# A two-layer diffusion step on one core: first norm, DeltaNet gate rounds and last products rearranged

## The chip, the cores and the metric

The kernel runs on one core of a Trainium2 chip. The core has five engines with a queue each: TensorE (PE, matmuls and transposes; PEld are its weight loads), VectorE (DVE), ScalarE (ACT), GpSimd (POOL) and SyncE (SP, which only starts DMA transfers). The metric is the device time of one execution in microseconds (us), the median of several runs. The rows below come from one profiled execution of the kernel before.

## What is computed

Two groups of tokens, 128 context tokens and 512 latent ones, run through two layers of width 1024 that share their weights: an attention layer, then a gated DeltaNet layer, each followed by a squared-ReLU MLP. What matters here, cut from the reference:

```python
def rms_norm(x, gain):
    y = x * lax.rsqrt(jnp.mean(x * x, axis=-1, keepdims=True) + EPS)
    return y * gain

def modulation(cond, w_mod, b_mod):                 # w_mod[l]: 1024 x 6144
    m = jax.nn.silu(cond) @ w_mod + b_mod
    return jnp.split(m[..., None, :], 6, axis=-1)   # shift1, scale1, gate1, shift2, ...

def trunk_layer(x, mods, gain1, gain2, w1, w2, mixer):
    shift1, scale1, gate1, shift2, scale2, gate2 = mods
    mix, aux = mixer(rms_norm(x, gain1) * (1 + scale1) + shift1)
    x = x + gate1 * mix
    h = rms_norm(x, gain2) * (1 + scale2) + shift2
    return x + gate2 * (jnp.square(jax.nn.relu(h @ w1)) @ w2), aux

def delta_mixer(h, ...):                            # 8 heads
    qkv, z, a, b = split(h @ w_in)                  # q, k, v: conv, SiLU; q, k normalised
    o = forward scan + backward scan                # chunked delta rule, per head
    o = rms_norm(o, norm_gain) * silu(z)            # z gates the head's output
    return o @ w_out

y = rms_norm(x, final_norm)                         # at the end, for both groups
```

## The kernel before

All 640 tokens are handled together: x is kept feature-major, 8 tiles of 128 features x 640 tokens. Matmuls take an fp32 operand as the sum of two halves: `split` has ACT write the rounded value (hi) and DVE or POOL the rest (lo), and `mm3` makes three matmuls of the two pairs. Tiles come from pools by tag: tag x has 12 slots, h and a 16 each, all of 128x640; `raw` has three and `wpair` six of 4 KB per partition. The code is handed to a scheduler that fixes the order of the instructions of each engine before the run; an engine works through its own list and waits at each row for what that row needs. SP's list of transfers is such a list too.

The stages, in the order of the program (`run`, L1322):

1. **The head.** Five token blocks of x are loaded (`xin`), `transpose_x` (L482) turns them feature-major with 40 PE transposes and 8 DVE copies, squares each x tile on ACT and adds the squares on DVE. Five pairs of PE matmuls with a column of ones give the sums per token, `finish_rstd` makes 1/rms of them on DVE (`rsy`), and PE spreads that over a PSUM tile (`big<-c,rsy`), called r0 here. Beside that, `modulate(0, 0, fetch_slots)` (L398) multiplies the two condition vectors with the first third of `w_mod[0]`: 32 transfers of 256 KB into slots of the tags h and a, 32 matmuls `mod<-...` of 512 columns; four of them stand at four places of the PE array (q = 0 to 3). `modulation` (L415) copies the result on ACT (`x<-mod`), transposes it back on PE and adds the bias and makes the gain on DVE. `columns` (L389) transposes the small constant vectors. `key_weights` (L572) splits the weights of the keys, one half on POOL and one on DVE, and those of query head 0 on POOL.
2. **The first norm**, `first_norm` (L506): DVE makes `us` = x * r0 (`a<-x,big`, 8 of 640 columns). Then, for three token segments (128, 256 and 256 tokens, each group with its own gain and shift) and 8 features each: a TENSOR_SCALAR u * gain + shift in place, ACT's rounded copy to hi, and the difference lo. For features 2 and 5 (f % 3 == 2) POOL does the first and the last step, else DVE.
3. **Attention.** Keys are made first (`attn_kv`, L578): 5 blocks of 24 matmuls `pd<-w,h` 128x256, which need all 24 tiles of h, block by block. The second third of `w_mod[0]` comes in through the `raw` slots, which the value weights hold before; its matmuls `S<-raw,c` are put between those of the keys. Then values, eight query heads, output.
4. **MLP 0**, then **DeltaNet** (`delta`, L1244) in rounds r = 0 to 10: round r weaves `dn_dense(r)`, `dn_decay(r-1)`, `dn_inverse(r-2)`, `dn_scan(r-3)` and `gated(ZROUNDS[r])`. `gated` makes z of a head (`dn_z`, 48 matmuls `pd<-h,w` 128x320, two ACT evacuations `x<-pd` 128x320 with SiLU) and then `dn_out` (L1221): ACT squares, a DVE chain, a product on POOL, five PE transposes, a DVE product, and a transfer to DRAM or a split. A head's output o stays in an a slot from its scan to its `dn_out`. In rounds 8 to 10 the other two thirds of `w_mod[1]` are woven in (`pd<-raw,c`, `pd<-a,c`).
5. **MLP 1**, with `final(0)` in the middle and `final(1)` at the end (L1398): for three token blocks, PE transposes two halves of 512 columns each; the first half is scaled by `rsy` and the final gain on DVE in one instruction, the second on ACT and then POOL. The transfers out stand on ACT's queue (first halves) and on SP's (second halves).

Of the kernel before, what the change touches and what calls it, by code (L numbers as in the profile page):

```python
# [15 lines left out]
P = 128  # L16
# [22 lines left out]
RSQRT_SEED = float(0x5F3759DF)  # L39
ZROUNDS = {6: (0,), 7: (1,), 8: (2, 3), 9: (4, 5), 10: (6, 7)}  # L40
MODS = (6, 6, 6)
# [78 lines left out]
class Model:  # L120
# [342 lines left out]

    def fetch_slots(self, src):
        out = []
        for i in range(4):
            r = self.main("h" if i < 2 else "a", shape=[P, 512])
            self.nc.sync.dma_start(out=r, in_=src[:, i * 512 : (i + 1) * 512])
            out.append(r)
        return out  # L470
# [10 lines left out]

    def transpose_x(self, xs, x):  # L482
        for f in range(FT):
            x.append(self.main("x"))
            ps = self.ps("big", 2, 1024)
            for b in range(NBLK):
                self.tr(ps[:, b * P : (b + 1) * P], xs[b][:, f * P : (f + 1) * P])
            self.nc.vector.tensor_copy(out=x[f], in_=ps[:, :T])
            sq = self.main("x")
            self.act(sq, x[f], AF.Square)  # L490
            if f == 0:
                acc = sq
            else:
                self.tt(acc, acc, sq, ALU.add)
            yield
        cols = self.ps("nps", 1)[:, :NBLK]
        for b in range(NBLK):
            self.mm(cols[:, b : b + 1], acc[:, b * P : (b + 1) * P], self.one_col)
        r = self.finish_rstd(cols)
        out = self.ps("big", 2, 1024)  # L500
        for b in range(NBLK):
            self.mm(out[:, b * P : (b + 1) * P], r[:, b : b + 1].to_broadcast([P, P]), self.ident)
        self.r0 = out[:, :T]
        yield

    def first_norm(self, x, gm):  # L506
        us = [self.main("a") for _ in range(FT)]
        for f in range(FT):
            self.tt(us[f], x[f], self.r0, ALU.mult)
        drain(gm)  # L510
        h = self.new_h()
        gain, mods = self.gains[0][0], self.mods[0]
        for s, e, g in FIRST:
            for f, (hi, lo) in enumerate(h):
                eng = self.nc.gpsimd if f % 3 == 2 else self.nc.vector
                u = us[f][:, s:e]
                self.ts(u, u, gain[:, f, g : g + 1], ALU.mult, mods[:, f, g : g + 1], ALU.add, eng=eng)
                self.act(hi[:, s:e], u, AF.Copy)
                self.tt(lo[:, s:e], u, hi[:, s:e].bitcast(F32), ALU.subtract, eng)
        return h  # L520
# [51 lines left out]
    def key_weights(self):  # L572
        v, g = self.nc.vector, self.nc.gpsimd
        self.kw = self.kv_weights(self.kv_raw(QW), lambda: self.wtile([P, 4, 256]), 4, (g, v))
        self.vraws = self.kv_raw(QW + KVH * P)
        self.q0 = self.pair(self.a["attn_w_in"][0], 0, 0, eng=g)

# [744 lines left out]
    def run(self):  # L1322
# [3 lines left out]
        FC = [f * P for f in range(FT)]  # L1326
        with psum("ps0") as self.pq:
            xs = self.load_x()
            self.setup()
            gm = self.modulate(0, 0, self.fetch_slots)  # L1330
            x = []
            tx = self.transpose_x(xs, x)
            for _ in range(FT):
                next(gm)
                next(tx)
            drain(tx)
            self.columns()
            self.key_weights()
            h = self.first_norm(x, gm)
        with pool("attn") as self.ph:  # L1340
# [36 lines left out]
        with pool("mlp1") as self.ph, psum("ps5") as self.pq:  # L1377
# [20 lines left out]
            def final(half):  # L1398
# [12 lines left out]
                for i, b in enumerate(blocks):  # L1411
                    y = self.wp.tile([P, D], F32, tag="wpair", bufs=self.NW, name=self.nm("y"))
                    for c in range(0, D, 512):
# [3 lines left out]
                        out = y[:, c : c + 512]  # L1417
                        if c == 0:
                            self.stt(out, ps, r[:, i : i + 1], gain[:, c : c + 512], ALU.mult, ALU.mult)
# [49 lines left out]
```

## Time and profile before

| | |
|---|---|
| runs shown | 1884.30, 1886.86, 1880.81 us; median 1884.3 us |
| the profiled execution, its own time | 1883.34 us |
| its span, first to last instruction | 1881.5 us (1.8 us of the time lie around it) |
| busy | PE 1793.3 us, DVE 991.3, ACT 753.9, POOL 311.6 |
| mean granted clock of TensorE | 0.984 of full speed |

The profile gives the start and length of each instruction on its engine, grouped where alike ones follow each other, and in brackets how long the engine stood idle before and whose work ended that. PEclk is the granted clock of TensorE: 1.00 is 2.4 GHz and 0.50 is 1.2 GHz. The span is nearly full of PE work, so the places of interest are those where PE has none: the head, short gaps in the DeltaNet rounds, and the tail.

### The profile page before, as it was taken

The numbers are of one execution on the slowest core, as the hardware profiler recorded it, in microseconds if no ns is written. First come the engines' busy times: TensorE is split into PE (matmuls) and PEld (weight loads), VectorE is DVE, ScalarE is ACT, GpSimd is POOL, SyncE is SP. The second block draws the span as 40 slices with busy tenths as digits, with TensorE's granted clock in tenths as the row PEclk, the third lists the DMA queues.
The fourth block names the chain that finished last, engine by engine and source line by source line (L and its number), as shares of the span: only waits on it lengthen the run. The fifth ranks groups of instructions, "written<-read, shape, count | busy, mean of one in ns | idle before, by whom it ended". The sixth has DMA issues, their size and how long they took to land.

```text
span 1881.5 us, 31040 instructions
## 1 busy us (share of the span) xinstructions
PE 1793.3 (95%) x11981; PEld 1657.3 (88%) x11981; DVE 991.3 (53%) x2294; ACT 753.9 (40%) x1725; POOL 311.6 (17%) x404
## 2 busy tenths in 40 slices
PE   6899999999999999999999999999899999999997
PEld 2778876979999999999898999776699999999997
DVE  4636662724454545556788876543664334343432
ACT  2445552523342433436766555533343223131331
POOL 1344221400010010142121101210251000000012
PEclk9899999999999999999999999999999999999998
DMA  7651127465676676624432332654721222222211
GB/s 279 217 161 49 34 85 219 112 201 165 189 224 196 198 227 180 200 82 165 130 105 81 106 109 85 192 169 143 230 81 48 74 79 74 73 79 75 72 46 56
DMA packets 289065, 248.84 MB, mean 132 GB/s; under 512 B 44847, under 2 KB 246982, under 8 KB 288918
## 3 DMA queue, kind: packets, MB, share of 16 engines
q1 hardware_dynamic: 269072, 207.85, 36.9%
q0 software_dynamic: 9136, 32.18, 4.7%
q10 hardware_dynamic: 10710, 6.83, 1.2%
q8 instruction: 94, 1.54, 0.3%
q14 instruction: 53, 0.43, 0.1%
HBM read 199.00 MB, written 45.20 MB: 130 GB/s over the span
## 4 chain that ended last, share of the span: by engine, by line
PE 75%; DVE 14%; DMA 5%; issue 2%; ACT 2%; POOL 1%; SPq 1%; POOLq 0%; ACTq 0%; DVEq 0%
PE dense L173 32%; PE pd L173 29%; PE scan L173 3%; PE big L173 2%; DVE cv L166 2%; PE mod L408 2%; DVE ptmp L160 2%; PE pd L408 2%; PE big L176 1%; DVE ptri L1069 1%; DVE a L160 1%; DMA raw<-in_w_mod 1%; DVE wide L160 1%; DMA ptmp<-gmd 1%; PE S L173 1%
## 5 line engine op out<-in xcount | busy, mean ns | idle before, releaser
L173 PE MATMUL pd<-h,w 128*128 128x320 f32 x2016 | 353.6, 320 | 10.3 <-ACT cv L163 6.2
L173 PE MATMUL dense<-a,wx 128*128 128x320 f32 x2238 | 338.4, 310 | 2.2 <-ACT wx L163 1.5
L173 PEld LDWEIGHTS dense<-a,wx 128*128 128x128 f32 x2238 | 331.6, 189 | 5.1 <-ACT wx L163 2.4
L173 PEld LDWEIGHTS pd<-h,w 128*128 128x128 f32 x2016 | 301.0, 190 | 37.0 <-issue 21.0
L163 ACT ACTIVATE wx<-raw 128x1024 fp32r<-128x1024 f32 x132 | 139.8, 1059 | 362.5 <-PE dense L173 214.7
L173 PE MATMUL dense<-h,wx 128*128 128x320 f32 x1776 | 266.9, 309 | 0.0
L173 PEld LDWEIGHTS dense<-h,wx 128*128 128x128 f32 x1776 | 261.7, 188 | 5.9 <-issue 5.0
L160 DVE TENSOR_TENSOR wx<-raw,wx 128x1024 fp32r<-128x1024 f32 x127 | 159.1, 1255 | 155.4 <-ACT wx L163 155.4
L173 PE MATMUL pd<-a,wx 128*128 128x320 f32 x1284 | 194.3, 309 | 0.0
L173 PEld LDWEIGHTS pd<-a,wx 128*128 128x128 f32 x1284 | 189.9, 188 | 0.0
L173 PE MATMUL pd<-h,wx 128*128 128x320 f32 x1008 | 152.0, 309 | 0.0
L166 DVE SCALAR_TENSOR_TENSOR x<-dense,c,x 128x192 f32<-128x192 f32 (+2 forms) x147 | 59.6, 433 | 175.3 <-PE dense L173 175.3
L173 PEld LDWEIGHTS pd<-h,wx 128*128 128x128 f32 x1008 | 148.8, 188 | 1.7 <-DVE a L160 1.7
L160 POOL TENSOR_TENSOR x<-x,half 128x320 f32<-128x320 f32 x48 | 54.1, 1127 | 526.1 <-ACT half L163 525.3
L163 ACT ACTIVATE a<-half 128x320 fp32r<-128x320 f32 x128 | 59.9, 471 | 112.5 <-DVE half L166 112.5
L160 DVE TENSOR_TENSOR a<-half,a 128x320 fp32r<-128x320 f32 x128 | 62.7, 492 | 65.2 <-ACT a L163 65.1
L911 POOL DMA_DIRECT2D wd<-w x58 | 31.0, 535 | 369.7 <-ACT w L163 289.8
L166 DVE SCALAR_TENSOR_TENSOR x<-pd,c,x 128x128 f32<-128x128 f32 (+2 forms) x87 | 35.8, 439 | 105.5 <-PE pd L173 105.4
L166 DVE SCALAR_TENSOR_TENSOR cv<-cv,c,cv 128x644 f32<-128x644 f32 x84 | 78.2, 931 | 20.0 <-ACT cv L163 18.9
L163 ACT ACTIVATE half<-x 128x320 f32<-128x320 f32 x56 | 26.0, 468 | 99.8 <-DVE x L166 99.8
L173 PE MATMUL big<-wide,a 128*128 128x128 f32 x480 | 64.4, 281 | 1.0 <-DMA wide<-td 0.8
L173 PEld LDWEIGHTS big<-wide,a 128*128 128x128 f32 x480 | 59.1, 194 | 5.8 <-ACT a L163 2.0
(294 smaller groups left out, 2510.9 us busy)
## 6 DMA issues: line engine op xcount, KB each, us to landing
raw<-in_mlp_w SPq DMA_DIRECT2D x128, 512.0 KB
wd<-w POOLq DMA_DIRECT2D x58, 512.0 KB, 4.4
w<-wd SPq DMA_DIRECT2D x58, 512.0 KB
raw<-in_w_mod SPq DMA_DIRECT2D x48, 512.0 KB
rawp<-in_dn_w_in SPq DMA_DIRECT2D x58, 256.0 KB
a<-in_w_mod SPq DMA_DIRECT2D x48, 256.0 KB
wm<-in_w_mod SPq DMA_DIRECT2D x16, 512.0 KB
raw<-in_attn_w_in SPq DMA_DIRECT2D x12, 512.0 KB
```

The source lines that it names most:

```text
L160: (eng or self.nc.vector).tensor_tensor(out=out, in0=in0, in1=in1, op=op)
L163: self.nc.scalar.activation(out=out, in_=in_, func=func, **kw)
L166: self.nc.vector.scalar_tensor_tensor(out=out, in0=in0, scalar=s, in1=in1, op0=op0, op1=op1)
L173: self.nc.tensor.matmul(out, l, r, start=first, stop=last)
L176: self.nc.tensor.transpose(out, in_, self.ident[:n, :n])
L408: nc.tensor.matmul(ps[32 * q : 32 * q + 32, :], self.cond[:, k, :], views[q], start=k == 0, stop=k == FT - 1, tile_position=(0, 32 * q),)
L911: self.nc.gpsimd.dma_start(out=d[z], in_=pair[z].bitcast(F32).rearrange("p k c -> p (k c)"))
L1069: nc.vector.tensor_reduce(out=t[:, BASE * i : BASE * i + i], in_=o, axis=AX.X, op=ALU.add)
```

## The change

Three parts. (1) The head: the squares are taken token-major, on ACT straight from `xin` with a running sum (`token_rstd`), so r0 no longer needs the feature-major tiles; `columns` stands ahead of the modulation; the first third of `w_mod[0]` goes into a pool of its own with 11 slots of 512 KB (16 transfers), and its matmuls are handed to the scheduler as issued after the last PE instruction traced so far (`tc.issue_after`); `first_norm` uses no POOL: ACT writes hi straight from u with its own scale and bias, DVE computes the same value into a tile t of tag x and then lo. The split of query head 0 moves from POOL to DVE and behind the first norm. (2) `ZROUNDS`: head 0's gate moves from round 6 to 7, 1 from 7 to 8, 3 from 8 to 9. (3) In `final`, the last token block's second half goes to DVE too.

```diff
@@ -37,7 +37,7 @@
 BASE = 16
 GROUP = 5
 RSQRT_SEED = float(0x5F3759DF)
-ZROUNDS = {6: (0,), 7: (1,), 8: (2, 3), 9: (4, 5), 10: (6, 7)}
+ZROUNDS = {7: (0,), 8: (1, 2), 9: (3, 4, 5), 10: (6, 7)}
 MODS = (6, 6, 6)
 DIRECT = 5
 NB = P // BASE
@@ -461,12 +461,12 @@
             out += [r[:, 0, :], r[:, 1, :]]
         return out
 
-    def fetch_slots(self, src):
+    def fetch_start(self, src):
         out = []
-        for i in range(4):
-            r = self.main("h" if i < 2 else "a", shape=[P, 512])
-            self.nc.sync.dma_start(out=r, in_=src[:, i * 512 : (i + 1) * 512])
-            out.append(r)
+        for i in range(2):
+            r = self.scr("wm", 11, [P, 2, 512])
+            self.nc.sync.dma_start(out=r, in_=src[:, i * 1024 : (i + 1) * 1024].rearrange("p (q c) -> p q c", q=2))
+            out += [r[:, 0, :], r[:, 1, :]]
         return out
 
     def load_x(self):
@@ -479,44 +479,42 @@
             xs.append(t)
         return xs
 
-    def transpose_x(self, xs, x):
+    def token_rstd(self, xs):
+        ss = self.small("sst", [P, NBLK], 1)
+        for b in range(NBLK):
+            junk = self.scr("junk", 1, [P, D])
+            self.act(junk, xs[b], AF.Square, accum_out=ss[:, b : b + 1])
+        r = self.finish_rstd(ss)
+        out = self.ps("big", 2, 1024)
+        for b in range(NBLK):
+            self.mm(out[:, b * P : (b + 1) * P], r[:, b : b + 1].to_broadcast([P, P]), self.ident)
+        return out[:, :T]
+
+    def transpose_x(self, xs):
+        x = []
         for f in range(FT):
             x.append(self.main("x"))
             ps = self.ps("big", 2, 1024)
             for b in range(NBLK):
                 self.tr(ps[:, b * P : (b + 1) * P], xs[b][:, f * P : (f + 1) * P])
             self.nc.vector.tensor_copy(out=x[f], in_=ps[:, :T])
-            sq = self.main("x")
-            self.act(sq, x[f], AF.Square)
-            if f == 0:
-                acc = sq
-            else:
-                self.tt(acc, acc, sq, ALU.add)
-            yield
-        cols = self.ps("nps", 1)[:, :NBLK]
-        for b in range(NBLK):
-            self.mm(cols[:, b : b + 1], acc[:, b * P : (b + 1) * P], self.one_col)
-        r = self.finish_rstd(cols)
-        out = self.ps("big", 2, 1024)
-        for b in range(NBLK):
-            self.mm(out[:, b * P : (b + 1) * P], r[:, b : b + 1].to_broadcast([P, P]), self.ident)
-        self.r0 = out[:, :T]
-        yield
-
-    def first_norm(self, x, gm):
+        return x
+
+    def first_norm(self, x, r0, gm):
         us = [self.main("a") for _ in range(FT)]
         for f in range(FT):
-            self.tt(us[f], x[f], self.r0, ALU.mult)
+            self.tt(us[f], x[f], r0, ALU.mult)
         drain(gm)
         h = self.new_h()
         gain, mods = self.gains[0][0], self.mods[0]
         for s, e, g in FIRST:
             for f, (hi, lo) in enumerate(h):
-                eng = self.nc.gpsimd if f % 3 == 2 else self.nc.vector
                 u = us[f][:, s:e]
-                self.ts(u, u, gain[:, f, g : g + 1], ALU.mult, mods[:, f, g : g + 1], ALU.add, eng=eng)
-                self.act(hi[:, s:e], u, AF.Copy)
-                self.tt(lo[:, s:e], u, hi[:, s:e].bitcast(F32), ALU.subtract, eng)
+                sc, sh = gain[:, f, g : g + 1], mods[:, f, g : g + 1]
+                t = self.main("x", shape=[P, 2 * SEQ])[:, : e - s]
+                self.act(hi[:, s:e], u, AF.Identity, scale=sc, bias=sh)
+                self.ts(t, u, sc, ALU.mult, sh, ALU.add)
+                self.tt(lo[:, s:e], t, hi[:, s:e].bitcast(F32), ALU.subtract)
         return h
 
     def spill(self, x, eng=None):
@@ -573,7 +571,6 @@
         v, g = self.nc.vector, self.nc.gpsimd
         self.kw = self.kv_weights(self.kv_raw(QW), lambda: self.wtile([P, 4, 256]), 4, (g, v))
         self.vraws = self.kv_raw(QW + KVH * P)
-        self.q0 = self.pair(self.a["attn_w_in"][0], 0, 0, eng=g)
 
     def attn_kv(self, h, x):
         nc, a = self.nc, self.a
@@ -1324,19 +1321,22 @@
         pool = lambda name: tc.tile_pool(name=name, bufs=1)
         psum = self.psum
         FC = [f * P for f in range(FT)]
-        with psum("ps0") as self.pq:
+        with pool("start") as self.ph, psum("ps0") as self.pq:
             xs = self.load_x()
             self.setup()
-            gm = self.modulate(0, 0, self.fetch_slots)
-            x = []
-            tx = self.transpose_x(xs, x)
-            for _ in range(FT):
-                next(gm)
-                next(tx)
-            drain(tx)
+            x = self.transpose_x(xs)
+            r0 = self.token_rstd(xs)
             self.columns()
+            tail = lambda: max(i for i, t in enumerate(nc.cur_bb.bb.instructions) if t.engine == PINNED[0])
+            traced = nc.cur_bb.bb.instructions
+            after = traced[tail()]
+            gm = self.modulate(0, 0, self.fetch_start)
+            with tc.issue_after(after):
+                for _ in range(FT):
+                    next(gm)
             self.key_weights()
-            h = self.first_norm(x, gm)
+            h = self.first_norm(x, r0, gm)
+            self.q0 = self.pair(a["attn_w_in"][0], 0, 0)
         with pool("attn") as self.ph:
             self.attention(h, x)
             first = self.prefetch(a["attn_w_out"][0], 0, FC)
@@ -1415,7 +1415,7 @@
                         for j in range(4):
                             self.tr(ps[:, j * P : (j + 1) * P], x[c // P + j][:, b * P : (b + 1) * P])
                         out = y[:, c : c + 512]
-                        if c == 0:
+                        if c == 0 or b == NBLK - 1:
                             self.stt(out, ps, r[:, i : i + 1], gain[:, c : c + 512], ALU.mult, ALU.mult)
                         else:
                             self.act(out, ps, AF.Copy, scale=r[:, i : i + 1])
```

Where instructions move, the order of an engine's list shows it. In these rows a name like `mod_227` is a tile and its number, and "x5" counts equal rows that follow each other.

TensorE in the head, around the matmuls of r0. Before (`nps_305` are the token sums of the squares, `big_325` is r0, `mod_121` the modulation's sum, `h_` and `a_` its weights):

```order
55 L408 MATMUL mod_121<-h_192,c_97 32x512
56 L408 MATMUL mod_121<-a_194,c_97 32x512
57 L173 MATMUL nps_305<-c_84,x_142 128x1 x5
58 L408 MATMUL mod_121<-a_196,c_97 32x512
59 L176 MATMUL nps_333<-c_82,a_101 128x128
60 L176 MATMUL nps_336<-c_82,a_102 128x128
61 L408 MATMUL mod_121<-h_213,c_97 32x512
62 L408 MATMUL mod_121<-h_215,c_97 32x512
63 L173 MATMUL big_325<-c_82,rsy_313 128x128
```

Now (`big_213` is r0, `mod_227` the modulation's sum, `wm_` its weights in the new pool):

```order
49 L408 MATMUL mod_227<-wm_238,c_100 32x512 x2
50 L408 MATMUL mod_227<-wm_244,c_100 32x512
51 L173 MATMUL big_213<-c_85,rsy_201 128x128 x5
52 L408 MATMUL mod_227<-wm_244,c_100 32x512
53 L408 MATMUL mod_227<-wm_246,c_100 32x512 x2
62 L408 MATMUL mod_227<-wm_284,c_100 32x512 x2
63 L408 MATMUL mod_227<-wm_286,c_100 32x512 x2
64 L176 MATMUL mod_326<-c_85,x_324 128x128 x4
65 L173 MATMUL pd_496<-w_296,h_335 128x256
```

The sums and the two transposes of `columns` are gone from this place, r0 comes behind the fifth of 16 weight tiles instead of among the matmuls of the fifth of eight row blocks of `w_mod`, each two such tiles, and the other 23 modulation matmuls follow it in one row.

GpSimd in the head. Before (`w_344` and `w_358` are lo halves of weights, `a_363` and `a_366` the features 2 and 5 of u, `h_393` and `h_399` their lo halves):

```order
15 L160 TENSOR_TENSOR w_344<-raw_339,w_343 128x1024
16 L170 TENSOR_SCALAR a_363<-a_363,c_117,c_115 128x128
18 L170 TENSOR_SCALAR a_363<-a_363,c_117,c_115 128x256
21 L170 TENSOR_SCALAR a_366<-a_366,c_117,c_115 128x256
22 L160 TENSOR_TENSOR h_393<-a_363,h_392 128x128
23 L160 TENSOR_TENSOR h_393<-a_363,h_392 128x256 x2
26 L160 TENSOR_TENSOR w_358<-raw_355,w_357 128x1024
27 L160 TENSOR_TENSOR h_399<-a_366,h_398 128x256
```

Now:

```order
13 L383 DMA a_105<-in_final_norm 8x128
14 L160 ISA
15 L160 TENSOR_TENSOR w_297<-raw_292,w_296 128x1024
16 L160 TENSOR_TENSOR dec_730<-a_717,a_461 128x512
17 L160 TENSOR_TENSOR dec_725<-dec_725,a_462 128x512
```

The first norm's rows and the second weight split have left GpSimd's list; they stand on VectorE.

ScalarE in DeltaNet, the evacuations of z. Before, in round 6 (`x_11551` is z of head 0):

```order
933 L163 ACTIVATE cv_11711<-pd_11712 128x128
934 L163 ACTIVATE cv_11711<-pd_11712 128x192
935 L163 ACT_TABLE_LOAD
936 L163 ACTIVATE x_11551<-pd_11552 128x320
937 L163 ACTIVATE a_11691<-big_11685 128x640
```

Now, the same place of round 6, and then round 9 (`x_13372` and `x_13558` are z of heads 3 and 4, `sso_13523` belongs to `dn_out`):

```order
927 L163 ACTIVATE cv_11668<-pd_11669 128x128
928 L163 ACTIVATE cv_11668<-pd_11669 128x192
929 L163 ACTIVATE a_11480<-scan_11731,ex_10460 128x128 x2
1086 L163 ACTIVATE x_13372<-pd_13373 128x320
1097 L163 ACTIVATE x_13372<-pd_13445 128x320
1102 L163 ACTIVATE x_13558<-pd_13559 128x320
1108 L163 ACTIVATE a_13524,sso_13523<-a_11480 128x128 x5
1111 L163 ACTIVATE x_13558<-pd_13618 128x320
```

Round 6 has no z any more, and round 9 has three where it had two; each z brings its 48 matmuls and a `dn_out` with it.

## Rows read from the trace of the kernel before

**Rows 1.** The page: busy time of the engines.

```profile
PE 1793.3 (95%) x11981; PEld 1657.3 (88%) x11981; DVE 991.3 (53%) x2294; ACT 753.9 (40%) x1725; POOL 311.6 (17%) x404
```

**Rows 2.** Windows: from:to, length, busy PE, PEld, DVE, ACT, POOL, clock, DMA share, GB/s.

```profile
42.85:48.06 5.21, 0.66 (x4) 0.42 (x4) 5.21 (x10) 3.00 (x4) 3.38 (x2) 0.76 0.02 6
48.06:58.21 10.15, 6.30 (x26) 5.73 (x26) 10.15 (x22) 5.73 (x18) 8.99 (x12) 0.62 0.96 339
58.21:73.50 15.29, 15.29 (x103) 13.34 (x104) 8.26 (x20) 7.97 (x31) 1.43 (x1) 0.89 0.53 180
```

**Rows 3.** DMA of 0 to 90 us: GB/s in 40 slices of 2.25 us.

```profile
GB/s 29 340 215 387 404 377 385 387 385 390 397 388 385 388 364 351 148 118 0 0 4 188 258 325 409 413 373 135 7 73 240 173 226 235 222 240 235 188 70 88
```

**Rows 4.** Timeline of the head: start, length, engine, instruction, count, idle before.

```profile
27.73 1.01 SPq L468 DMA_DIRECT2D a<-in_w_mod  x2
...
39.24 5.94 DVE L160 TENSOR_TENSOR a<-x,big 128x640 f32<-128x640 f32 x8 [4.78 <-PE big L173]
...
42.85 0.60 ACT L163 ACTIVATE x<-mod 128x512 f32<-128x512 f32 x1 [14.14 <-PE mod L408]
...
43.50 0.66 PE L176 MATMUL mod<-c,x 128*128 128x128 f32 x4 [0.75 <-ACT x L163]
...
46.78 1.21 DVE L160 TENSOR_TENSOR w<-raw,w 128x1024 fp32r<-128x1024 f32 x1
...
47.91 0.22 DVE L166 SCALAR_TENSOR_TENSOR c<-c,c,c 128x8 f32<-128x8 f32 x1
...
48.06 0.84 DVE L170 TENSOR_SCALAR a<-a,c,c 128x128 f32<-128x128 f32 x3
```

**Rows 5.** Group of VectorE, 48 to 66 us: count, busy us, mean ns.

```profile
L170 DVE TENSOR_SCALAR a<-a,c,c 128x256 f32<-128x256 f32 x12 | 7.7, 665 | 0.0
```

**Rows 6.** Timeline of VectorE, end of the first norm.

```profile
57.88 0.28 DVE L160 TENSOR_TENSOR h<-a,h 128x128 fp32r<-128x128 f32 x1
...
62.15 0.40 DVE L170 TENSOR_SCALAR a<-a,c,c 128x256 f32<-128x256 f32 x1
...
65.43 0.42 DVE L160 TENSOR_TENSOR h<-a,h 128x256 fp32r<-128x256 f32 x1
```

**Rows 7.** Timeline of TensorE, the matmuls of the keys.

```profile
51.89 4.23 PE L173 MATMUL pd<-w,h 128*128 128x256 f32 x18 [1.03 <-POOL h L160]
58.21 11.58 PE L173 MATMUL pd<-w,h 128*128 128x256 f32 x82 [2.09 <-DVE h L160]
69.72 1.05 PE L408 MATMUL S<-raw,c 128*32 128x512 f32 x4
```

**Rows 8.** Windows of the DeltaNet rounds 6, 8 and 9, columns as in rows 2.

```profile
1070.00:1125.00 55.00, 52.67 (x387) 51.45 (x386) 42.07 (x121) 29.61 (x93) 7.31 (x16) 0.97 0.34 102
...
1181.00:1237.00 56.00, 51.87 (x348) 39.20 (x348) 31.02 (x109) 30.34 (x112) 12.79 (x12) 1.00 0.66 195
1237.00:1290.00 53.00, 50.82 (x315) 36.23 (x314) 21.31 (x76) 17.36 (x59) 5.24 (x5) 1.00 0.46 148
```

**Rows 9.** Timeline of the tail.

```profile
1869.93 1.41 DVE L166 SCALAR_TENSOR_TENSOR y<-dense,rsy,fgain 128x512 f32<-128x512 f32 x2
...
1870.74 3.79 POOL L160 TENSOR_TENSOR y<-y,fgain 128x512 f32<-128x512 f32 x3 [7.12 <-ACT y L163]
...
1872.04 2.85 SPq L1424 DMA_DIRECT2D out_y_sample<-y  x3
```

**Rows 10.** Chain of waits in round 8: modulation matmuls alone and side by side.

```profile
1202.57 0.98 PE pd L408 x2
...
1206.62 1.00 PE pd L408 x8
```

**Rows 11.** SP's list: the tiles of x written to DRAM.

```profile
50.54 6.35 SPq L525 DMA_DIRECT2D xs<-x  x8
```

**Rows 12.** Chain of waits: 48 matmuls of 320 columns in MLP 1.

```profile
1421.89 7.04 PE pd L173 x48
```

**Rows 13.** Waits of TensorE, 1300 to 1360 us: total, times, longest.

```profile
PE big L176 <- DVE a L160: 6.9, 1, 6.9
```

## The prediction, made before the changed kernel was run

> **What bounds the kernel now.** I began with the page: TensorE is busy for 1793.3 of 1881.5 us [rows 1], so an edit pays where TensorE has nothing to do or where its matmuls wait in a row for another engine. The windows of the first 75 us show such a place [rows 2]: from 42.85 to 48.06 TensorE works 0.66 us, and from 48.06 to 58.21 it works 6.30 of 10.15 us at a mean clock of 0.62, while VectorE is busy without a break and GpSimd for 8.99 us. Only after 58.21 does TensorE run full. Next the transfers: the rate is steady at 380 to 400 GB/s until about 34 us and zero around 41 to 45 us [rows 3]. So the early transfers set nothing after 34 us.
>
> Then the timeline [rows 4]. SyncE starts the last piece of `w_mod` by 28.74 us, yet ScalarE copies the modulation's result (`x<-mod`) only at 42.85, because TensorE takes its list in order and the last modulation matmuls stand behind the matmuls of r0, which wait for the squares, sums and 1/rms. After r0, VectorE makes the eight u products from 39.24 to 45.18; the gains come at 47.91 and the first norm starts at 48.06. There VectorE is the bound: its TENSOR_SCALAR of 256 columns takes 665 ns on average [rows 5], but 0.40 us when GpSimd has no work; the last lo ends at 65.43 + 0.42 = 65.85 us [rows 6]. The keys' 120 matmuls follow it: 18 of them take 4.23 us early on (0.235 each), 82 take 11.58 us from 58.21 (0.141 each), the modulation's matmuls come between them from 69.72 [rows 7], and the keys end near 73.5, where the last window ends [rows 2].
>
> In DeltaNet TensorE idles 2.3 us of round 6, 4.1 of round 8 and 2.2 of round 9 (length less busy) [rows 8]. At the end, VectorE's three products start at 1869.93, GpSimd's three take 3.79 us from 1870.74, and SyncE's last issue ends at 1872.04 + 2.85 = 1874.9 [rows 9].
>
> **The head.** All of x (five pieces of 512 KB, 2.6 MB) and the first third of `w_mod` (8.4 MB) are 11.0 MB. Summing the rates slice by slice gives 10.9 MB at 31.5 us [rows 3], so the last weight can be there at 32 us. The change takes the squares off the transposed tiles and puts r0 behind the fifth of 16 weight tiles; nothing behind it in TensorE's list waits for more than a transfer. The 32 modulation matmuls, four side by side, cost about 1 us a group where all is there [rows 10], while the 1 MB of a group takes 2.7 us to arrive at 387 GB/s; so they keep up, and the result is there at 33 instead of 42.85. VectorE has made u by then, because r0 no longer stands behind anything late. What follows: the copy 0.60, the transposes 0.66, sums 0.25 and gains 0.22 [rows 4], with hand-overs about 2 us. The first norm starts at 35, which is 13 us earlier.
>
> It then has more on VectorE: 24 TENSOR_SCALARs and 24 lo differences, and two weight splits of 1.21 [rows 4]. By their lengths without GpSimd [rows 6]: 16 x (0.40 + 0.42) = 13.1; 8 x (0.28 + 0.28) = 4.5, the TENSOR_SCALAR of 128 columns at three in 0.84 us [rows 4]; 2.4 for the splits. That is 20.0 us, and I add 1 us for the one split that GpSimd keeps beside it. The last lo is done at 56, 9.9 us earlier. ScalarE's hi halves read u and run ahead of it; they cost nothing while VectorE is the bound. The added table load and five squares of ScalarE lie under the arriving x.
>
> Behind that stand the last 24 key matmuls (3.4 us at 0.141) and two groups of modulation matmuls (1.05 each [rows 7]), 5.5 us: 61.5. One wait is added. The order puts the first of these groups behind the 106th key matmul. Its weights go into `raw` slots that the value weights hold until VectorE splits them, right after the last lo. Between the issue of the last early weight and its arrival lie some 3.3 us (28.74 to 32); with issue and splits that is between 0 and 4 us of standing still, and I take 2. The keys end at 63.5 instead of 73.5: **-10**, bounds -12 and -6 (the latter at the lower clock, below). The tiles t of the third segment use slots of x that become free when x is written to DRAM, eight transfers in 6.35 us [rows 11]; in SyncE's new list they stand behind VectorE's first weight split, so they begin near 41 and are out as VectorE gets there, at 46: nothing taken, up to 2 us if they are late.
>
> **The gates.** One z is 48 matmuls of 320 columns, 7.04 us [rows 12]. Round 6 loses one and round 9 gains one, with its `dn_out`; rounds 7 and 8 keep their number. Round 6 works 52.67 us on TensorE and 42.07 on VectorE [rows 8], so without z they are 45.6 and 42.07 and fit into 48: it loses 7.0, of which I give 0.7 back for gaps that z used to fill. Round 9 grows by 7.0 less its idle 2.2. The reordered rounds also set the modulation matmuls of layer 1 side by side less often: counted in the order, 39 groups' worth for 36, and a lone one costs as much (0.98) as four together (1.00): +2.9. Sum -6.3 + 4.8 + 2.9 = +1.4, taken as **+1.5**. Bounds: -4 if round 8's and 9's gaps (6.3) are filled and the groups cost 1; +8 if round 6 keeps its length.
>
> **The tail.** VectorE makes four products of 0.71 from 1869.93, done at 1872.8; GpSimd makes two of 1.27, done at 1873.3 instead of 1874.53 [rows 9]. The last issue comes 0.9 to 1.2 us earlier: **-0.9**, bounds 0 and -1.3.
>
> **Sum.** The profiled execution took 1883.34 us (span 1881.5 and 1.8 around it), 1.0 below the median of 1884.3. 1883.34 - 10 + 1.5 - 0.9 = 1873.9, so **1874**.
>
> **A rule against it.** After the stretch in which TensorE works 0.66 of 5.21 us, the mean granted clock is 0.62, nearer to 1.2 than to 2.4 GHz [rows 2], and 18 key matmuls cost 0.235 us each [rows 7]. The Trainium skill, "TensorE: Matmul & The Clock Gate", Part 1: The HAM clock gate, says that the throttled state is the default and that activity releases it. By that rule the keys, which VectorE feeds slowly in the new kernel too, could stay at 1.2 GHz throughout. What that gives by rows is the second rival. I take the higher clock for the last 24 matmuls, since the 82 of rows 7 averaged 0.141.
>
> **The rivals.**
>
> 1. The forecast: head -10, gates +1.5. It comes to 1871 to 1877. Chance 0.50.
> 2. The keys stay at 1.2 GHz: 120 x 0.235 = 28.2 us from 36, 64.2, and two groups at 1.9 each: 68, a gain of 5.5 only; 1883.3 - 5.5 + 1.5 - 0.9 = 1878.4. Against it: those 82 matmuls. Chance 0.16.
> 3. More on both: no stop for the `raw` slots and the gaps of rounds 8 and 9 filled: -12 - 2 - 1.3 gives 1868. For it: the idle in rows 8. Chance 0.15.
> 4. Round 6 keeps its length, since the work that it weaves around z waits on VectorE: gates +8, 1883.3 - 10 + 8 - 0.9 = 1880.4. Against it: VectorE's 42 us. Chance 0.08.
> 5. The change doesn't bring the modulation forward: the new pool has 11 slots for 16 tiles, and if TensorE frees them late, behind copies of VectorE, the last five come late. If the result comes at 38, half the gain is lost: 1879. Against it: five tiles need only the first five to be used. Chance 0.07.
> 6. Slower: head 1's and 3's outputs stay in an a slot one round longer; if a tile of rounds 7 to 9 then has to wait for a `dn_out` to free one, TensorE waits through a chain like that at the end of DeltaNet, 6.9 us [rows 13]. Three of them: 1874 + 20.7 = 1894.6. It decides from losses of 15.9 us on, that is from the third; the order shows no such wait, and the slots are not counted there. Chance 0.04.
>
> **How the numbers follow.** A measurement of this kernel tells some 0.3%, 5.65 us, from no change: faster is below 1878.65, slower above 1889.95. Faster: all of 1 and 3, about half of 2, a fifth of 5 and a little of 4, 0.76; slower: 6, and a mishap not named, 0.04; same 0.20. The range 1864 to 1883 holds 1, 2, 3, 5 and most of 4; its own ends are the head at -12 with the gates at -4 and the tail at -1.3 (1866), with 2 us for what is not seen, and the sum of 4 with 2.6 us.
>
> **What would show it.** In the changed kernel's profile `x<-mod` stands near 33 and the first TENSOR_SCALAR of the first norm near 35; GpSimd has one TENSOR_TENSOR in the head; the last lo ends near 56, the keys near 63.5; round 6 is shorter by some 6 us, round 9 longer by 5; SyncE's last issue stands 1 us closer to VectorE's first product. The prediction is wrong if the clock of the keys' stretch stays at 0.5 to its end, if `x<-mod` comes after 36, or if round 6 is as long as before.

## The result and the profile after

The changed kernel took 1874.45 us (median of 7 runs, 1871.64 to 1877.13) against 1884.11 for the kernel before on the same chip: ratio 0.995, 95% interval 0.9937 to 0.9963, or 7.0 to 11.9 us less. The forecast was 1874, with -10 for the head, +1.5 for the gates and -0.9 for the tail. The total is right; the parts are less so.

The page of the changed kernel's profiled execution (1876.26 us, span 1874.5), against [rows 1]:

```profile
PE 1786.5 (95%) x11971; PEld 1654.7 (88%) x11971; DVE 989.5 (53%) x2301; ACT 757.4 (40%) x1727; POOL 297.7 (16%) x390
```

GpSimd has lost 13.9 us of work and TensorE 6.8 us of busy time, though of its matmuls only the ten small ones of the sums have gone (11981 to 11971). The mean granted clock rose from 0.984 to 0.986, so part of what it lost can be time at the lower clock.

The timeline of the head, against [rows 4], [rows 6] and [rows 7]:

```profile
28.20 0.33 SPq L468 DMA_DIRECT2D wm<-in_w_mod  x1
...
33.65 1.05 PE L408 MATMUL mod<-wm,c 128*32 128x512 f32 x4 [1.19 <-DMA wm<-in_w_mod]
34.75 0.60 ACT L163 ACTIVATE x<-mod 128x512 f32<-128x512 f32 x1 [22.16 <-PE mod L408]
...
36.30 2.46 DVE L166 SCALAR_TENSOR_TENSOR c<-c,c,c 128x8 f32<-128x8 f32 x2
36.38 2.36 POOL L160 TENSOR_TENSOR w<-raw,w 128x1024 fp32r<-128x1024 f32 x1 [28.02 <-ACT w L163]
...
38.69 1.10 DVE L170 TENSOR_SCALAR x<-a,c,c 128x128 f32<-128x128 f32 x4
...
52.47 7.21 PE L173 MATMUL pd<-w,h 128*128 128x256 f32 x58 [1.40 <-ACT blk L163]
...
56.28 0.43 DVE L160 TENSOR_TENSOR h<-x,h 128x256 fp32r<-128x256 f32 x1
...
60.29 1.05 PE L408 MATMUL S<-raw,c 128*32 128x512 f32 x4 [0.61 <-DMA raw<-in_w_mod]
61.28 1.22 PE L173 MATMUL pd<-w,h 128*128 128x256 f32 x8
62.85 1.05 PE L408 MATMUL S<-raw,c 128*32 128x512 f32 x4 [0.35 <-DMA raw<-in_w_mod]
63.83 0.97 PE L173 MATMUL pd<-w,h 128*128 128x256 f32 x6
64.64 1.04 PE L173 MATMUL pd<-h,w 128*128 128x320 f32 x6
```

The modulation's result is copied at 34.75 instead of 42.85, the first norm starts at 38.69 instead of 48.06, and the next stage's first matmul (`pd<-h,w`) stands at 64.64. In the kernel before, the same timeline has it at 73.55, so the keys end 8.9 us earlier:

```profile
73.55 0.84 PE L173 MATMUL pd<-h,w 128*128 128x320 f32 x4
```

The last weight tile (SyncE, 28.20) lets its matmuls start only at 33.65, and between copy and first norm lie 3.9 us, in which VectorE's two gain instructions of 8 columns take 2.46 us, as long as GpSimd's product beside them.

The windows of that stretch (columns as in [rows 2]):

```profile
34.75:38.69 3.94, 1.20 (x5) 0.67 (x5) 2.60 (x5) 2.03 (x3) 2.31 (x1) 0.81 0.61 203
38.69:44.00 5.31, 4.27 (x14) 3.32 (x14) 4.75 (x15) 5.20 (x11) 0.05 (x1) 0.50 0.67 203
44.00:48.00 4.00, 4.00 (x21) 3.84 (x21) 3.93 (x14) 4.00 (x10) 0.00 (x0) 0.57 1.01 356
48.00:52.47 4.47, 2.64 (x18) 2.04 (x17) 4.47 (x14) 4.47 (x14) 0.00 (x0) 1.00 1.00 394
52.47:60.00 7.53, 7.21 (x58) 7.01 (x58) 7.05 (x17) 4.99 (x20) 0.00 (x0) 1.00 0.33 83
```

After a stretch with 1.20 us of work in 3.94 the granted clock falls to 0.50 (1.2 GHz), and from 48 us on it is 1.00 (2.4 GHz).

In DeltaNet, ScalarE's rows `cv<-cv,c` 128x644 are the first tap of a convolution. Each head has three; the third marks where the dense matmuls of its round end. Here are the third rows of the last three heads (rounds 5, 6 and 7) and the last evacuation of a gate. Timeline of ScalarE, before:

```profile
1068.05 0.83 ACT L163 ACTIVATE cv<-cv,c 128x644 f32<-128x644 f32 x1
...
1123.30 0.83 ACT L163 ACTIVATE cv<-cv,c 128x644 f32<-128x644 f32 x1
...
1179.69 0.83 ACT L163 ACTIVATE cv<-cv,c 128x644 f32<-128x644 f32 x1
...
1332.15 0.42 ACT L163 ACTIVATE x<-pd 128x320 f32<-128x320 f32 x1
```

And after:

```profile
1063.93 0.83 ACT L163 ACTIVATE cv<-cv,c 128x644 f32<-128x644 f32 x1
...
1112.10 0.83 ACT L163 ACTIVATE cv<-cv,c 128x644 f32<-128x644 f32 x1
...
1166.43 0.83 ACT L163 ACTIVATE cv<-cv,c 128x644 f32<-128x644 f32 x1
...
1328.06 0.42 ACT L163 ACTIVATE x<-pd 128x320 f32<-128x320 f32 x1
```

Round 6 takes 48.2 us instead of 55.3, round 7 54.3 instead of 56.4, and the rest 161.6 instead of 152.5: what two rounds win (9.1) the later ones give back (9.2).

The tail, against [rows 9]:

```profile
1864.14 1.41 DVE L166 SCALAR_TENSOR_TENSOR y<-dense,rsy,fgain 128x512 f32<-128x512 f32 x2
...
1864.96 2.49 POOL L160 TENSOR_TENSOR y<-y,fgain 128x512 f32<-128x512 f32 x2 [7.14 <-ACT y L163]
...
1866.12 0.74 DVE L166 SCALAR_TENSOR_TENSOR y<-dense,rsy,fgain 128x512 f32<-128x512 f32 x1
1866.26 2.06 SPq L1424 DMA_DIRECT2D out_y_sample<-y  x3
```

From VectorE's first product to the end of the span it is 1874.5 - 1864.14, or 10.3 us with the unrounded span, where it was 1881.5 - 1869.93 = 11.6.

### The profile page after: what moved, and what is told of

It is laid out like the page before. It is cut to its first block, busy times and chain, and to the rows that moved or that the text cites. A ratio compares the mean times of both kernels' runs of the same rounds, so it can differ in the third digit from the quotient of the medians.

```text
span 1874.5 us, 31001 instructions
## 1 busy us (share of the span) xinstructions
PE 1786.5 (95%) x11971; PEld 1654.7 (88%) x11971; DVE 989.5 (53%) x2301; ACT 757.4 (40%) x1727; POOL 297.7 (16%) x390
## 4 chain that ended last, share of the span: by engine, by line
PE 75%; DVE 12%; DMA 6%; ACT 2%; issue 2%; POOL 1%; SPq 1%; ACTq 0%; POOLq 0%; DVEq 0%
PE dense L173 33%; PE pd L173 29%; PE scan L173 3%; PE big L173 3%; DVE ptmp L160 2%; PE pd L408 2%; PE mod L408 1%; DMA wide<-gd 1%; DMA raw<-in_w_mod 1%; PE big L176 1%; DVE ptri L1066 1%; DVE cv L166 1%; DMA wm<-in_w_mod 1%; PE S L173 1%; DVE pv L160 1%
## 5 line engine op out<-in xcount | busy, mean ns | idle before, releaser
L173 PE MATMUL big<-wide,a 128*128 128x128 f32 x480 | 63.5, 278 | 1.2 <-DMA wide<-td 0.9
```

The source lines that it names most:

```text
L173: self.nc.tensor.matmul(out, l, r, start=first, stop=last)
```

## The experiments

**The three parts alone.** The first is the changed kernel with the old rounds and last products, the other two are the kernel before with one line changed:

```diff
-ZROUNDS = {6: (0,), 7: (1,), 8: (2, 3), 9: (4, 5), 10: (6, 7)}
+ZROUNDS = {7: (0,), 8: (1, 2), 9: (3, 4, 5), 10: (6, 7)}
```

```diff
-                        if c == 0:
+                        if c == 0 or b == NBLK - 1:
```

> The kernel before with the head's part of the change alone (rounds and last products as before). Theory (the head is the whole gain, and what it wins at the keys stays won): the keys end near 64.6 us as in the changed kernel, the attention runs some 8 us earlier, the time is 1875 to 1877. Rival (half of the head's 8 us is given back between the attention and DeltaNet, for a cause that belongs to the change): DeltaNet starts only 5 us earlier and the time is about 1879.

> The kernel before with the new rounds of the gates alone. Theory: 1 to 1.5 us slower, 1885, since TensorE works the same and only the modulation groups stand alone more often; round 7 ends some 8 us earlier and round 9 gives it back. Rival (the later gates fill TensorE's gaps in rounds 8 and 9): 2 to 4 us faster, 1880 to 1882.

> The kernel before with the fourth last product on VectorE alone. Theory: from VectorE's first last product to the end of the span 10.4 us instead of 11.6, 1.2 us won, 1883. Rival (the last transfer is bound by the other queue's issues): 11.6 as before, 1884.

Head alone: 1872.97 us, ratio 0.9957 (0.9938 to 0.9977), the keys' end at 64.94 (changed kernel 64.64). Gates alone: 1881.18, 0.9992 (0.9976 to 1.0009). Tail alone: 1884.71, 1.0008 (0.9992 to 1.0023); its end stands 1884.2 - 1873.90 = 10.3 us behind VectorE's first product. So the head is the whole gain that the times can tell, and it is not half lost by DeltaNet: the table further below has head alone 10.7 us ahead there. The tail's 1.3 us are there in each of the ten profiles that have it (10.3, against 11.6 in the four without it) and are too small for the total. Of the gates neither theory is borne out by this run alone.

**GpSimd's weight split in the head.**

```diff
-        self.kw = self.kv_weights(self.kv_raw(QW), lambda: self.wtile([P, 4, 256]), 4, (g, v))
+        self.kw = self.kv_weights(self.kv_raw(QW), lambda: self.wtile([P, 4, 256]), 4, (v, v))
```

> The changed kernel with the one weight split that GpSimd keeps in the head given to VectorE too, so that GpSimd has no work there. Theory (the two gain instructions, 2.46 us long in the changed kernel, are held by GpSimd's product beside them): they take 0.2 us each, the first norm starts at 36.7 instead of 38.69, the last lo ends near 56 (1.9 won, 1.2 for the added split), the time is 0 to 1 us less than the changed kernel. Rival (they wait for something else): 2.4 us as before, the last lo ends 1.2 us later, near 58.

Timeline of this run, the gain instructions, the first norm's start, and the matmul behind the keys:

```profile
35.92 0.36 DVE L166 SCALAR_TENSOR_TENSOR c<-c,c,c 128x8 f32<-128x8 f32 x2
36.20 1.11 DVE L170 TENSOR_SCALAR x<-a,c,c 128x128 f32<-128x128 f32 x4
```

```profile
63.11 1.04 PE L173 MATMUL pd<-h,w 128*128 128x320 f32 x6
```

The two take 0.36 us instead of 2.46, and although VectorE has one split more, the keys end at 63.11 instead of 64.64. The theory holds: GpSimd's product held VectorE. Two runs further below, in which that product comes later, agree: the gains take 0.37 us there, and in one of them three TENSOR_SCALARs of 128x128, which now stand beside the product (2.34 us), take 2.98. The Trainium skill, "GPSIMD Engine Reference", 8. Key points, says that the two engines share their interfaces to the on-chip memory and contend where VectorE reads two inputs from it; the gain instruction reads two, and this run agrees. In total 1875.26 (ratio 0.9954, 0.9938 to 0.997): no difference that can be told from the changed kernel.

**When the last weights can arrive.** Rows 6 and 7 of the eight row blocks go to free h slots:

```diff
-            views = ahead or get(k)
+            views = ahead or (get(k) if early or l or slab or k < 6 else self.fetch_h(self.a["w_mod"][l, k * P : (k + 1) * P, :2048]))
```

> The changed kernel with the last two of the eight row blocks of the early modulation weights fetched into eight free slots of tag h (256 KB each), so that no weight tile past the eleventh but the twelfth waits for a slot of the new pool. Theory (in the changed kernel the last tile is issued only at 28.2 us because its slot comes free late, and then shares the rate with the key weights): the last weights are issued before 27 us, the copy of the modulation's result stands at 33.0 to 33.5 instead of 34.75, the keys end 1 us earlier, near 63.7. Rival (the transfers are bound by their bytes alone): the copy stays at 34.5 or later.

```profile
35.40 0.60 ACT L163 ACTIVATE x<-mod 128x512 f32<-128x512 f32 x1 [21.04 <-PE mod L408]
```

The copy came later, not earlier; the keys ended at 65.24. The theory falls. But the 0.65 us by which the copy is later were there before: r0's first matmul stands at 26.52 here and at 25.84 in the changed kernel, and from it to the copy both take 8.9 us. In the changed kernel the rate falls to 311 GB/s from 27 to 28 us, where the slot is waited for, and to 226 from 31 to 32; here it stays above 340 until 36, and the last weights came no earlier. When the last matmuls could start, 11.8 MB had been moved there (352 GB/s for 33.65 us) and 12.0 here (350 for 34.3), of which x and the early weights are 11.0: part of the rate at the end goes to the key weights that are issued behind them.

**What the first norm's new body does.** First the features 2 and 5 back on GpSimd in the changed kernel; then the new body alone in the kernel before; then the changed kernel with the old body:

```diff
+                eng = self.nc.gpsimd if f % 3 == 2 else self.nc.vector
-                self.ts(t, u, sc, ALU.mult, sh, ALU.add)
-                self.tt(lo[:, s:e], t, hi[:, s:e].bitcast(F32), ALU.subtract)
+                self.ts(t, u, sc, ALU.mult, sh, ALU.add, eng=eng)
+                self.tt(lo[:, s:e], t, hi[:, s:e].bitcast(F32), ALU.subtract, eng)
```

> The changed kernel with features 2 and 5 of the first norm back on GpSimd (first and last step). Theory (VectorE without GpSimd beside it loses little by the added quarter): the last lo ends within 1.5 us of the changed kernel's 56.7, the keys end at 64 to 66, so that the gain of the head is that of the earlier start, not of the emptied GpSimd. Rival (GpSimd's share was what held the keys): the last lo ends at 60 or later and the keys at 68 or later.

> The kernel before with the first norm's new body alone (no GpSimd in it, the rounded half straight from u, query head 0's split behind it), with the squares and the modulation as before. Theory: the first norm starts near 48 as before and is bound by VectorE's 20 us of work, the last lo ends at 66 to 68, the keys end at 73 to 76: nothing won. Rival (the emptied GpSimd is the gain): the keys end at 69 or earlier.

> The changed kernel with the old body of the first norm (features 2 and 5 on GpSimd, gain and shift in place, hi as a copy of the result, query head 0's split on GpSimd), so that only the early token sums, the early r0 and the weights' own pool are left of the head's part. Theory (the earlier start is the gain; the body adds little): the copy of the modulation's result stands near 34.7 and the keys end 25 to 26 us after the first TENSOR_SCALAR as before, at 63 to 66 us. Rival (GpSimd's share delays the keys, as when features 2 and 5 were put back): 70 us or later.

With features 2 and 5 on GpSimd, the timeline and the waits of TensorE:

```profile
61.95 1.92 PE L408 MATMUL S<-raw,c 128*32 128x512 f32 x4 [4.97 <-DMA raw<-in_w_mod]
...
75.94 1.48 PE L173 MATMUL pd<-h,w 128*128 128x320 f32 x9
```

VectorE's last lo ended at 57.0, as the theory had it, but the keys at 75.94: both expectations failed in part. The scheduler had set six modulation groups ahead of the keys' end instead of two, and the first of them stood 4.97 us for weights whose slots the value weights held. That is an order, not GpSimd's speed: in the third run, with the old body whole, no group stands there, and the keys end at 63.17, 25.8 us after the first TENSOR_SCALAR, as its theory had it. But the groups must be done before the first scores, and that is where bodies can be compared. Old body, then the changed kernel:

```profile
104.87 1.05 PE L408 MATMUL S<-raw,c 128*32 128x512 f32 x4 [1.60 <-DMA raw<-in_w_mod]
107.59 1.92 PE L408 MATMUL S<-raw,c 128*32 128x512 f32 x4 [1.67 <-DMA raw<-in_w_mod]
...
110.98 3.40 PE L173 MATMUL S<-key,x 128*128 128x320 f32 x12
```

```profile
107.39 2.00 PE L173 MATMUL S<-key,x 128*128 128x320 f32 x12
```

The kernel before has them at 116.16. So the changed kernel is 8.8 us ahead by there, and the old body with the early start 5.2. The other 3.6 can't all be put to the new body. In the run with the old body r0's first matmul stood 1.1 us later than in the changed kernel (26.98 against 25.84), before either body begins. From the copy to the first scores that run takes 75.5 us, and the one with features 2 and 5 on GpSimd 75.2 (scores at 111.41). The changed kernel, its second profile and head alone take 72.6 to 73.5, but the three kernels with the old head and the old body take no longer, 72.6 to 73.3. In the run with the old body two modulation groups wait 1.60 and 1.67 us for weights there, where the changed kernel has one such wait, of 1.50. The gain at the first scores is therefore the earlier copy; the 2 to 3 us that GpSimd's share costs with the early start are not told apart from the order that the scheduler makes for it. At the start of DeltaNet (below) the run with the old body was 8.0 us ahead of the kernel before, so that the 3.6 did not show there.

The new body alone in the kernel before (1879.99 us in one run, beside 1886.22):

```profile
39.36 0.60 ACT L163 ACTIVATE x<-mod 128x512 f32<-128x512 f32 x1 [11.79 <-PE mod L408]
```

```profile
69.46 0.45 PE L173 MATMUL pd<-h,w 128*128 128x320 f32 x2
```

Neither expectation is met: the last lo ended at 61.1 and the keys 4.1 us earlier than before, and the reason is not where either looked: up to the copy this run has the kernel before's order, and yet the copy stands at 39.36 instead of 42.85 [rows 4], 3.5 us earlier. So 0.6 at most is the body's at the keys (and some 1 us at the first scores, 72.1 us behind the copy against 72.6 to 73.3). For the 3.5, the timeline's row of the sums' first matmul and one window (columns as in [rows 2]), this run and then the kernel before:

```profile
28.48 1.28 PE L173 MATMUL nps<-c,x 128*128 128x1 f32 x10 [0.77 <-DVE x L160]
```

```profile
34.00:36.00 2.00, 2.00 (x14) 1.12 (x16) 0.25 (x1) 0.00 (x0) 0.00 (x0) 1.00 1.07 346
```

```profile
29.63 1.28 PE L173 MATMUL nps<-c,x 128*128 128x1 f32 x10 [0.78 <-DVE x L160]
```

```profile
34.00:36.00 2.00, 2.00 (x7) 0.69 (x4) 0.40 (x3) 0.00 (x0) 0.00 (x0) 0.50 1.12 352
```

1.15 us stand there before the sums, at the full clock in both, and stay unexplained. From the sums to the copy it is 10.88 us here at the full clock and 13.22 before, where the clock stood at 0.50 from 32 to 38 us; in gates alone and tail alone, which fell too (0.55 there), it is 13.2 as well. These 2.3 us go with the clock.

**The lower clock at the keys.** Six matmuls of 512 columns that nobody reads keep TensorE busy:

```diff
+                if l == 0 and slab == 0 and k == FT - 1 and q == 2:
+                    spare = self.ps("nps", 1)
+                    for i in range(2):
+                        self.mm(spare[:, :512], self.ident, views[i])
...
+        if l == 0 and slab == 0:
+            spare = self.ps("nps", 1)
+            for i in range(4):
+                self.mm(spare[:, :512], self.ident, m)
```

> The changed kernel with six added TensorE matmuls of 512 columns whose results nobody reads: two ahead of the last four modulation matmuls, four behind the transposes of the modulation's result, where TensorE waits for the first norm. Theory (the lower clock between 38.7 and 48 us costs little, because the keys' end is set by VectorE's last lo, by the evacuations and by the modulation weights that come after): the granted clock between 41 and 48 is above 0.9 and the keys end within 0.7 us of the changed kernel's 64.6. Rival (the lower clock sets the keys' end): they end 1.5 to 3 us earlier.

Windows, and the matmul behind the keys:

```profile
41.00:44.00 3.00, 1.74 (x10) 1.06 (x8) 2.96 (x9) 3.00 (x8) 0.00 (x0) 1.00 0.73 228
44.00:48.00 4.00, 3.46 (x21) 2.74 (x22) 3.86 (x14) 4.00 (x9) 0.00 (x0) 1.00 0.92 287
53.00:56.00 3.00, 2.90 (x13) 2.90 (x14) 3.00 (x11) 1.34 (x7) 0.00 (x0) 0.50 0.36 138
```

```profile
66.71 0.46 PE L173 MATMUL pd<-h,w 128*128 128x320 f32 x2
```

The clock is 1.00 where it was 0.50 and 0.57, and at the full clock TensorE only waits for VectorE there instead of working slowly. But it fell later, to 0.50 from 53 to 56 us, where the changed kernel has 1.00. The keys' end moved by 2.1 us, more than I had written: r0 stood 1.3 us later in this run (27.13), and the added matmuls take up to 0.7 more before the copy, at 36.69. From the copy to the keys' end it is 30.0 us, as in the changed kernel (64.64 - 34.75 = 29.9). So the rival, 1.5 to 3 us won, falls, but the run does not show the keys at the full clock throughout. What such a stretch costs is seen better in the second profile of the changed kernel (below): it has the copy at 34.75 too and a lower clock from 54 to 57 us besides. This profile first, then the first one:

```profile
54.00:57.00 3.00, 3.00 (x16) 3.00 (x16) 3.00 (x7) 0.07 (x1) 0.00 (x0) 0.50 0.03 5
```

```profile
54.00:57.00 3.00, 3.00 (x27) 3.00 (x26) 3.00 (x7) 1.32 (x6) 0.00 (x0) 1.00 0.02 5
```

Its keys end at 65.11 instead of 64.64: the 11 matmuls that are missing in this stretch cost 0.5 us, since the two waits for the `raw` weights (0.61 and 0.35) are gone in exchange.

**The old gates again, beside the changed kernel.**

> The changed kernel with the old rounds of the gates. Theory (the new rounds cost 1 to 2 us, by the modulation groups that stand alone): 1 to 2 us less than the changed kernel on the same chip; the stretch from the first convolution's copy at 872 to the last gate's evacuation is 455 us instead of 456. Rival (the new rounds gain): 1 to 3 us more.

> The changed kernel with the old rounds of the gates and with no work for GpSimd in the head. Theory (both act where the single runs showed them): keys end near 63.1 us as in the run without GpSimd, and the time is 2 to 3 us less than the changed kernel on the same chip, about 1871 to 1872. Rival (the gain at the keys is lost again at the transfers behind them): no difference beyond the interval.

> The changed kernel once more, on the same chip as the two above, so that they can be compared with it. Expected: 1872 to 1877.

On one chip, 5 rounds each: changed kernel 1875.11 (ratio to before 0.9956), with the old gates 1874.18 (0.9953), with the old gates and no GpSimd in the head 1873.08 (0.9951; its keys end at 63.35). The intervals are some 3 us to either side: no version beats the changed kernel by more than can be measured. The stretch from the first row `cv<-cv,c` (871.92 in the changed kernel) to the last gate's evacuation was 453.6 to 458.3 us in the six profiles with old gates, mean 455.9, and 454.2 to 456.5 in the eight with new ones, mean 455.4. Neither the theory's cost nor the rival's gain shows: the 0.5 us between the means is less than the spread of either group, so the move is worth nothing here that can be told.

The five kernels that ran once, with times from 1869.3 to 1880.0 us, are read by their profiles alone: runs of the changed kernel itself lie between 1868.1 and 1879.3. And no run takes the early sums, the places of r0 and `columns`, and the pool of the weights apart; what each of them is worth by itself is not shown.

## Why the prediction was right, step by step

**The modulation's copy at 33: 34.75.** The order did what I said. The term that was too small is the arrival of the last weight, which I had put at 32 from the bytes of x and `w_mod` alone. In the trace its last packet (of 4 KB) ends at 33.1, and 0.4 MB of the key weights (packets of 1 KB), issued behind it, are moved before that. In the kernel before the last packet of `w_mod` ended at 33.3: the change won and lost nothing there, and giving slots away did not help.

**Two us to the first norm: 3.9.** This is the step that failed. I priced the gains at 0.22 each, from the one that stood alone in [rows 4]; the other, beside GpSimd's split, stood in the same timeline of the kernel before, and I had left it out:

```profile
45.30 1.55 DVE L166 SCALAR_TENSOR_TENSOR c<-c,c,c 128x8 f32<-128x8 f32 x1
```

With GpSimd empty the two take 0.36, and the norm starts 1.8 us after the copy.

**VectorE's 21 us: 18.0**, from 38.69 to 56.71. The shapes cost what their rows said (0.41 and 0.43 for 256 columns), but instructions that follow each other overlap: two of 0.41 take 0.74. A sum of lengths from rows of single instructions is too long by that, here by 2 us of my 20. The 1 us added for GpSimd's split was not spent here at all: the split ran beside the gains. It was luck that this error of 3 us covered most of the two before it (1.75 and 1.9), and so the last lo, forecast at 56, ended at 56.7. The transfers of x began at 43.62 instead of 41, and VectorE waited for none of them, as I had taken it.

**The keys' end at 63.5: 64.64**, 8.9 us won of 10. Behind the last lo I had 24 key matmuls; 37 were left (43 in the kernel before). TensorE had lost time earlier, in a wait that I had not seen: 1.40 us for ScalarE's evacuation (`blk`), which stands behind the hi halves and a weight's rounding in its list. I had called the hi halves free. From there on it made 58 key matmuls in 7.21 us and waited for no lo any more, so the last lo did not set the end, as I had it. Against that, the wait for the `raw` slots that I put at 2 was 0.61 + 0.35. The two errors nearly cancel: 7.9 us from the last lo to the end, where I had 7.5.

**The lower clock**, the second rival: it came, down to 0.50 until 47 us, but the keys did not stay there. My price of 28.2 us multiplied all 120 matmuls by the slow length; 28 or so ran at it, while VectorE was still making their operands. What it cost is at most half a us as far as the runs show.

**The gates: +1.5, measured -0.5, which is not told from 0.** Round 6 lost 7.1 (I had 6.3), and the later rounds gave back 9.2, for round 7's 2.1 too. That the modulation groups would cost 2.9 us is not seen.

**The tail: -0.9, measured -1.3.** VectorE's first product to the end, 10.3 us instead of 11.6, in every profile.

**Between the parts.** The sum held because the head gained 8 to 9 instead of 10 and the gates cost nothing: that these two errors have opposite signs is luck. In a single profile that is hidden by what the next table shows: by how much a VectorE instruction starts earlier than the same one in the profile of the kernel before, at five times of that kernel (us; minus is earlier).

| run | 127 | 292 | 335 | 399 | 862 |
|---|---|---|---|---|---|
| changed kernel | -8.1 | -8.0 | -7.1 | -4.7 | -5.1 |
| the same, second profile | -8.2 | -8.5 | -8.7 | -8.8 | -9.2 |
| head alone | -7.5 | -9.6 | -9.6 | -10.3 | -10.7 |
| old body | -4.5 | -7.7 | -7.6 | -7.1 | -8.0 |
| gates alone | -0.6 | +1.5 | +1.3 | +5.2 | +5.2 |
| tail alone | -0.4 | -2.2 | -2.0 | +1.4 | +1.4 |

The last two rows have the kernel before's order of instructions up to 862 and yet differ from it by 5.2 and 1.4 us. So "half of the head's gain is lost by DeltaNet", as the first profile alone would have it, is not a property of the change: the second profile has 9.2 there, and head alone and the changed kernel with the old gates, whose order is the same up to there, have 10.7 and 8.5.

## What to carry to other kernels

Move the reduction that a long row of other work stands behind off that row: here the result at the end of the row, the copy, came at 34.3 to 36.7 us in the ten profiles with the early sums, and at 42.0 to 42.9 in three of the four without (39.4 in the fourth). Price an instruction by the row where its neighbours are as they will be, above all VectorE beside GpSimd, and price a run of alike instructions by the row that shows several of them. Before a difference of a few us is read from two profiles, look at how far two profiles of the same code differ.

## What the runs showed of the hardware

The granted clock of TensorE fell at some places in some executions and not in others, with the same instructions. Windows of the start of MLP 0, changed kernel and then its second profile:

```profile
352.00:362.00 10.00, 8.98 (x43) 8.98 (x44) 4.69 (x14) 2.33 (x3) 0.86 (x1) 0.66 0.68 188
340.00:400.00 60.00, 56.33 (x327) 45.63 (x326) 28.33 (x58) 20.23 (x41) 18.72 (x21) 0.94 0.55 174
```

```profile
340.00:400.00 60.00, 56.34 (x346) 44.29 (x344) 29.47 (x58) 21.36 (x42) 17.53 (x19) 1.00 0.59 187
```

In both TensorE stands still just before, for 2.4 us up to 353.0 and up to 351.7, where it waits for the norm. The dip at 352 goes with 2.4 us lost between 335 and 399 in the table; the second profile lost nothing there, and gates alone, with a clock of 0.91 from 340 to 400, lost 3.9. The start of MLP 1 went the other way: 0.83 in the changed kernel, 0.66 in the kernel before:

```profile
1401.00:1411.00 10.00, 9.47 (x57) 9.37 (x58) 5.72 (x17) 2.26 (x4) 0.47 (x1) 0.83 0.60 172
```

```profile
1405.00:1415.00 10.00, 9.08 (x43) 9.08 (x44) 4.70 (x14) 2.26 (x3) 0.86 (x1) 0.66 0.63 184
```

The keys, from 54 to 57 us, are a third place (0.50 and 1.00, shown above), and the chain of sums and r0 in the old head a fourth: 0.50 to 0.55 from 32 to 38 us in three profiles, 1.00 in another, 2.3 us apart. In all ten profiles with the new head TensorE ran at the full clock there (1.00 from 28 to 34.5 us); why is not shown.
